# Two of the four sums of down weights, moved from the gate/up stage into the down stage; accumulating transfers in turn; GpSimd without ordered waits on VectorE

## The chip, the cores and the metric

The kernel runs on one core of one Trainium2 chip. The metric is the device time of an execution in microseconds (us). The kernel before takes 2027.6 us, the median of three runs (2026.89 to 2027.85).

The engines are called as the profile calls them: PE is TensorE (matmul), PEld its weight loads, DVE is VectorE, ACT is ScalarE, POOL is GpSimd, and SP is the engine whose queue issues most DMA transfers.

## The reference

Two layers of a decoder trunk on 1024 tokens of width 1024, in float32. Each layer normalises, projects, runs four token mixers side by side, projects back and adds; then comes a feed-forward block of inner width 2816. The change lies in that block alone:

```python
h2 = rmsnorm(x, ffn_norm[l])
gate, up = jnp.split(h2 @ w_gate_up[l], 2, axis=-1)
x = x + (jax.nn.silu(gate) * up) @ w_down[l]
```

The accuracy asked for is that of float32.

## The kernel before, in words

**Products.** A float32 matrix is split into a high part that PE takes as it is and a low part, the rest. `split` does that: a cast on ACT for the high part, a subtraction on DVE for the low one. A product of two matrices is then three matmuls (high by high, high by low, low by high), issued by `mm3`; all matmuls of this kind have one line in the profile, L350. So each weight goes through load, cast, subtraction, matmul, in this order, and each step is an instruction on another engine.

**Seven products instead of eight.** Both products of the feed-forward block are cut into 2 x 2 blocks and done by a scheme with seven block products, named B11, B21, N1, N2, T3, T4 and B22. Each product multiplies one combination of weight blocks with one combination of activation blocks. Some combinations are blocks as they are, others are sums.

*The gate/up stage* goes through 22 column groups f. Per f, it needs sums of the gate/up weights. For f from 3 on, POOL makes them in SBUF (`GateUp.sums` and `sum4`, L1336 to L1338 and L1361). For the first three, 0, 1 and 2, they are made ahead of time in DRAM tiles `gd` by DMA transfers issued from POOL's queue, some of which add to what the destination holds (`gu_made`, L324). Layer 1's `gd` is made during layer 0's gate/up stage, one transfer per f (`next(made_next, None)`, L1705); each transfer is made to wait for the last matmul issued so far (`paced`). POOL also multiplies in the silu (L1545).

*The down stage* goes through 28 units: the seven combinations in the order B11, B21, N1, N2, T3, T4, B22, four column groups m in each. A unit is 33 matmuls. Its weight is a tile of 128 x 1408 (`Wide`: a pair of 512 columns and a half of 384). `dn_raw` issues a unit's loads two units ahead, and `dn_weights` splits them one unit ahead. The activations come back from DRAM tiles `ad`.

**Where the sums of down weights are made before.** Four of the seven combinations need a sum of the four stored blocks w0 to w3: N1 needs w2 + w3, N2 needs that and w0, T3 needs w2 + w0, B22 needs that of N2 and w1. During gate/up groups f = 4 to 19 (`DN_SUMS`), each step takes a quarter of one m: `dn_load` loads 352 columns of the four blocks, `dn_sum` makes the four sums with four POOL additions of 128 x 352 (L1623) and stores them to the DRAM tile `qd`. In the down stage, `dn_raw` reads each of the four straight from `qd`, so that POOL has nothing to do there.

**What sets the order.** The program is traced once; then the class `Order` lays out the instructions of all engines with a list of costs, chooses the order on each engine, the PSUM banks and the SBUF slots (48 pairs), tries variations, and fixes the result as a chain on each engine (`impose`). On top of that, `turns` gives many POOL additions one more wait: for the DVE operation that ends just before the addition's planned start. Any change in the program lets the planner find a new order for all of it.

Of the kernel before, what the change touches and what calls it, by code (L numbers as in the profile page):

```python
# [17 lines left out]
ALU = mybir.AluOpType  # L18
# [5 lines left out]
L = 2  # L24
HT = 512
# [9 lines left out]
B11, B21, B22, N1, N2, T3, T4, B12 = range(8)  # L35
# [93 lines left out]
def trunk_kernel(ctx: ExitStack, tc: tile.TileContext, ins, out, given=None, ends=None):  # L129
    nc = tc.nc  # L130
    act, dve, pe, pool, sp = nc.scalar, nc.vector, nc.tensor, nc.gpsimd, nc.sync
# [9 lines left out]
    R, F = View(slots, F32R), View(slots, F32)  # L141
# [155 lines left out]
    last_mm = None  # L297

    def paced(d):

        tc.add_manual_dep(
            d.ins,
            last_mm.ins.name,
            mybir.DependencyInfo(mybir.DependencyClass.Sync, mybir.DependencyReason.DATA),
            reason="pace",
        )

    def gu_made(l):

        for f in made[l]:  # L310
            w, o = ins["w_gu"][l, f], made[l][f]
            q = o.rearrange("p (n c) -> p n c", n=4)
            a11, a22, a21 = w[0, :, :HT], w[0, :, HT:], w[1, :, HT:]
            two = lambda a: a.unsqueeze(1).to_broadcast([P, 2, HT])
            for d, a, add in (
                (q[:, :2], two(a21), None),
                (o[:, : 2 * HT], w[0], ALU.add),
                (o[:, 2 * HT :], w[1], None),
                (q[:, 2:], two(a22), ALU.add),
                (q[:, 2:], two(a11), ALU.add),  # L320
                (o[:, 2 * HT : 3 * HT], a21, ALU.add),
            ):
                more = {} if add is None else {"accum_op": add}
                paced(pool.dma_start(d, a, **more))  # L324
                yield

# [193 lines left out]
    for l in range(L):  # L520
# [1010 lines left out]
        acts = {}  # L1531
        made_next = gu_made(l + 1) if l + 1 < L else iter(())
        pending = None
# [66 lines left out]
        def dn_raw(c, m):  # L1600
            w = Wide(F)
            q = {N1: 3, N2: 0, T3: 2, B22: 1}
            src = qd[m][q[c]] if c in q else ins["w_dn"][l, m, {B11: 0, B21: 1, T4: 3}[c]]
            for o, cs in zip(w.parts(), (slice(0, 2 * HT), slice(2 * HT, KW))):
                sp.dma_start(o, src[:, cs])
            return w

        CW = KW // 4

        def dn_load(n):  # L1610

            m, cs = n // 4, slice(n % 4 * CW, n % 4 * CW + CW)
            q = F.pair(), F.pair()
            for i in range(2):
                src = ins["w_dn"][l, m, 2 * i : 2 * i + 2, :, cs]
                sp.dma_start(slots.cur[q[i] // 2][:, :, :CW], src.rearrange("q p n -> p q n"))
            return m, cs, q

        def dn_sum(m, cs, q):

            w0, w1, w2, w3 = (F.ap(i + n)[:, :CW] for i in q for n in range(2))
            for o, a, b in ((w3, w2, w3), (w2, w2, w0), (w0, w3, w0), (w1, w0, w1)):
                pool.tensor_tensor(out=o, in0=a, in1=b, op=ALU.add)  # L1623
            for i in range(2):
                o = qd[m][2 * i : 2 * i + 2, :, cs]
                sp.dma_start(o.rearrange("q p n -> p q n"), slots.cur[q[i] // 2][:, :, :CW])
                F.free_pair(q[i])

# [69 lines left out]
        for f in range(3, NFF):  # L1698
# [5 lines left out]
            if l + 1 < L:  # L1704
                next(made_next, None)  # L1705
            if f % 2:
                g = f // 2
                sp.dma_start(ad_of(B11, g), F.ap(acts[2 * g][HALVES.index(0)]))
# [192 lines left out]
class Order:  # L1901
# [241 lines left out]

    def turns(self, order):

        end, _ = self.run(None, fixed=order)
        start = [x - s for x, (s, _) in zip(end, self.cost)]
        two = [k for k in order["DVE"] if self.kind[k] == "two"]
        pairs, i = [], 0
        for g in order["Pool"]:  # L2150
            if self.kind[g] != "pool":
                continue
            d = None
            while i < len(two) and end[two[i]] <= start[g] + self.LEAST:
                d = two[i]
                i += 1
            if d is not None:
                pairs.append((d, g))
        return pairs

    def trial(self, order):
# [73 lines left out]
    @staticmethod  # L2235
    def impose(tc, traced, order, turns):
        for a, b in turns:
            tc.add_manual_dep(
                traced[b],
                traced[a].name,  # L2240
                mybir.DependencyInfo(mybir.DependencyClass.Sync, mybir.DependencyReason.DATA),
                reason="turn",
            )
        for ks in order.values():
# [11 lines left out]
def scheduled_kernel(fresh, ins_of, rounds=1):  # L2256

    def trace(banks, ends, order=None, turns=()):  # L2260
        nc = fresh()
        ins, out = ins_of(nc)
        with tile.TileContext(nc) as tc:
# [6 lines left out]
            if order is not None:  # L2270
                Order.impose(tc, traced, order, turns)
        return nc, traced, asked
# [3 lines left out]
    for slow in SLOW:  # L2276
        plan, asked, first.slow = first, tried, slow
        end = plan.find()[2]
        for _ in range(rounds):
# [5 lines left out]
            order = plan.improve(best, 30)[1]  # L2285
            found.append((plan.trial(order), given, order, plan.turns(order)))
    best = min(found, key=lambda x: x[0])
    return trace(*best[1], *best[2:])[0]


# [133 lines left out]
```

## Time and profile before

| | |
|---|---|
| runs, median (lowest to highest) | 2027.6 us (2026.89 to 2027.85) |
| the profiled execution's own time | 2027.71 us |
| its span | 2025.9 us |
| granted TensorE clock, mean | 0.999 |
| bytes read from and written to HBM | 248.71 MB, 111.67 MB |
| layer 0: gate/up, down | about 390 to 793 us, 793 to 1012 |
| layer 1: gate/up, down | about 1390 to 1793 us, 1793 to 2017 |

The span runs from the first to the last instruction; the rest of the time, 1.8 us, lies around it. In a table of stretches, the columns after the stretch are its length and then, for each engine, the us it was busy and (x) how many instructions began; PEclk is the granted clock, 1.00 being full speed, and the last two are the mean busy share of the 16 DMA engines and what they moved in GB/s. In a row of a group, the mean in ns of one instruction stands behind the busy time, and behind the second bar the idle time just before the group's instructions, with what ended most of it. In a row of waits stand the total, the number and the longest. A matmul's end is modelled and overlaps the next one, so a row of PE can be 100% busy and still lose a tenth of a microsecond here and there.

### The profile page before, as it was taken

Reading aid. Unit: us, or ns where it says so; the run is one execution under the profiler, and the core shown is the slowest. Engines: PE = TensorE matmul, PEld = TensorE weight load, DVE = VectorE, ACT = ScalarE, POOL = GpSimd, SP = SyncE. Lnnn points to the kernel's source line nnn. Section 1 sums busy time; section 2 is a strip of 40 time slices with the busy share of each in tenths; the row PEclk is TensorE's granted clock in tenths of the full one; section 3 lists DMA queues with packets and bytes.
Section 4 is the critical chain, followed back from the end, with each engine's and each line's share of the span. In section 5 each row is a group of like instructions: output and inputs, shape, how many; then the busy total and the mean of one; then the engine's idle time right before and its main releaser. Section 6 shows DMA issues by size and latency. Waiting matters only on the chain.

```text
span 2025.9 us, 26778 instructions
## 1 busy us (share of the span) xinstructions
PE 2012.9 (99%) x9394; PEld 1672.9 (83%) x9394; DVE 1515.0 (75%) x2330; ACT 1026.4 (51%) x1772; POOL 529.9 (26%) x440
## 2 busy tenths in 40 slices
PE   9999999999999999999999999999999999999998
PEld 8888888888888888888888888888888888888887
DVE  8889978987667778776646898789866666676554
ACT  8457657843333335545533676677433333354343
POOL 0110000047776773000000000000577676610000
PEclk9999999999999999999999999999999999999999
DMA  6552233347666677998822133342454554487552
GB/s 209 109 105 62 72 104 112 120 154 210 203 210 197 199 210 261 386 346 299 279 75 66 48 94 127 101 154 89 164 184 165 201 172 168 163 314 250 189 177 84
DMA packets 157336, 345.91 MB, mean 171 GB/s; under 512 B 15248, under 2 KB 62480, under 8 KB 157200
## 3 DMA queue, kind: packets, MB, share of 16 engines
q1 hardware_dynamic: 150480, 326.88, 47.0%
q0 software_dynamic: 6720, 17.30, 5.2%
q8 instruction: 74, 1.21, 0.2%
q14 instruction: 62, 0.51, 0.1%
HBM read 248.71 MB, written 111.67 MB: 178 GB/s over the span
## 4 chain that ended last, share of the span: by engine, by line
PE 94%; DVE 4%; issue 1%; ACT 1%; DMA 1%; POOL 0%; DVEq 0%; SPq 0%; POOLq 0%; ACTq 0%
PE ps_mm L350 36%; PE ps_s L350 29%; PE ps_t L350 11%; PE ps_pv L350 8%; PE ps_pv L1163 2%; PE ps_t L1151 2%; PE ps_s L1093 1%; PE ps_s L1094 1%; PE ps_s L1095 1%; PE ps_s L687 1%; DVE u L373 1%; PE ps_pv L765 1%; PE ps_t L753 1%; PE ps_t L430 1%; PE ps_s L964 0%
## 5 line engine op out<-in xcount | busy, mean ns | idle before, releaser
L350 PE MATMUL ps_mm<-u,u 128*128 128x512 f32 (+1 forms) x3412 | 837.8, 389 | 1.8 <-DVE tm L451 1.2
L350 PEld LDWEIGHTS ps_mm<-u,u 128*128 128x128 f32 x3412 | 623.1, 188 | 125.4 <-DVE tm L451 2.0
L373 DVE TENSOR_TENSOR u<-u,u 128x1024 fp32r<-128x1024 f32 (+3 forms) x465 | 499.1, 1095 | 191.8 <-ACT u L370 156.6
L350 PE MATMUL ps_s<-u,u 128*128 128x512 f32 x2604 | 620.3, 389 | 0.0
L370 ACT CAST u<-u 128x1024 fp32r<-128x1024 f32 (+3 forms) x465 | 393.3, 864 | 405.6 <-DMA u<-ad 76.7
L350 PEld LDWEIGHTS ps_s<-u,u 128*128 128x128 f32 x2604 | 488.6, 188 | 102.9 <-DVE u L1412 0.6
L350 PE MATMUL ps_t<-u,u 128*128 128x512 f32 (+1 forms) x1080 | 244.9, 377 | 0.1
L350 PEld LDWEIGHTS ps_t<-u,u 128*128 128x128 f32 x1080 | 194.4, 188 | 38.0 <-DVE u L1380 0.4
L350 PE MATMUL ps_pv<-u,u 128*128 128x512 f32 x792 | 191.6, 390 | 0.2 <-ACT tm L1441 0.2
L1160 POOL MEMSET u<- 128x128 f32 x32 | 6.3, 222 | 699.6 <-PE ps_mm L350 467.8
L350 PEld LDWEIGHTS ps_pv<-u,u 128*128 128x128 f32 x792 | 148.4, 188 | 32.0 <-ACT tm L1441 0.6
L1545 POOL TENSOR_TENSOR tm<-tm,u 128x512 f32<-128x512 f32 x76 | 108.8, 1432 | 119.8 <-DVE u L373 56.8
L1543 ACT ACTIVATE tm<-tm 128x512 f32<-128x512 f32 x76 | 48.1, 633 | 131.9 <-DVE tm L451 131.9
L370 ACT CAST u<-ps_t 128x512 fp32r<-128x512 f32 (+3 forms) x132 | 64.5, 503 | 51.2 <-PE ps_t L1151 26.0
L1623 POOL TENSOR_TENSOR u<-u,u 128x352 f32<-128x352 f32 x64 | 79.4, 1242 | 29.9 <-DVE u L373 12.3
L373 DVE TENSOR_TENSOR u<-ps_t,u 128x512 fp32r<-128x512 f32 (+3 forms) x132 | 74.9, 582 | 15.0 <-ACT u L370 13.8
L1441 ACT COPY tm<-ps_s 128x512 f32<-128x512 f32 x62 | 36.3, 586 | 86.7 <-PE ps_s L350 77.5
L414 ACT ACTIVATE tm<-u 128x512 f32<-128x512 f32 (+1 forms) x91 | 53.7, 599 | 46.6 <-DVE u L1807 37.8
L324 POOL DMA_DIRECT2D gd<-in_w_gu x36 | 32.0, 889 | 167.6 <-PE ps_t L350 63.3
L375 ACT ACTIVATE u<-u,par 128x512 fp32r<-128x512 f32 x91 | 63.8, 716 | 19.4 <-DVE u L451 10.7
L451 DVE TENSOR_TENSOR tm<-tm,u 128x512 f32<-128x512 f32 x76 | 71.8, 945 | 2.2
L1623 POOL TENSOR_TENSOR u<-u 128x352 f32<-128x352 f32 x64 | 69.9, 1095 | 13.4 <-DVE u L373 6.5
(205 smaller groups left out, 2287.6 us busy)
## 6 DMA issues: line engine op xcount, KB each, us to landing
u<-in_w_gu SPq DMA_DIRECT2D x82, 512.0 KB, 3.8
ad<-u SPq DMA_DIRECT2D x154, 256.0 KB, 2.8
u<-ad SPq DMA_DIRECT2D x70, 512.0 KB, 6.1
u<-in_w_dn SPq DMA_DIRECT2D x64, 352.0 KB, 3.4
qd<-u SPq DMA_DIRECT2D x64, 352.0 KB, 2.4
u<-in_w_in SPq DMA_DIRECT2D x43, 512.0 KB, 4.7
u<-qd SPq DMA_DIRECT2D x32, 512.0 KB, 5.9
gd<-in_w_gu POOLq DMA_DIRECT2D x30, 512.0 KB, 6.8
```

The lines of the kernel that those rows point to most:

```text
L350: last_mm = pe.matmul(o, w, r, start=start and k == 0 and i == 0, stop=stop and k == n - 1 and i == 2, skip_group_check=again,)
L370: a = act.copy(hi, f)
L373: dve.tensor_tensor(out=lo, in0=f, in1=rd(hi), op=ALU.subtract)
L375: a = act.activation(hi, f, AF.Copy, scale=gain)
L414: act.activation(q, f, AF.Square)
L451: dve.tensor_tensor(out=o, in0=a, in1=b, op=ALU.mult)
L1151: pe.transpose(p[:, b * P : (b + 1) * P], pr[b][j // 4][:, (j % 4) * P : (j % 4 + 1) * P], ident,)
L1163: pe.matmul(py[:, c0:], v_of(j, h), R.ap(s)[:, c0:], start=j == 0 and n == 0, stop=j == nj - 1 and n == 1,)
L1441: act.copy(o, p)
L1543: last_silu = act.activation(g, g, AF.Silu)
L1545: pool.tensor_tensor(out=g, in0=g, in1=r, op=ALU.mult)
L1623: pool.tensor_tensor(out=o, in0=a, in1=b, op=ALU.add)
```

## The change

It does three things.

1. `dn_load` and `dn_sum` now make two of the four sums in the gate/up stage: w2 + w3 and, from it, w0 + w2 + w3. A step loads three blocks instead of four and does two additions of 128 x 352 instead of four (L1640 in the new file). The other two sums are made in the down stage: for T3 and B22, `dn_raw` loads two wide tiles instead of one, and POOL adds the second to the first in three pieces of 512, 512 and 384 columns (L1621).
2. The accumulating transfers for layer 1's `gd` go in turn: the first transfer of each of the three groups, then the second of each, and so on, instead of all six of one group after another. Each waits for the matmul that was the last one a group f earlier (`past`), not for the latest.
3. `turns` is taken out: POOL's additions no longer wait for a DVE operation unless their data or their slot asks for it.

```diff
+    def gu_made(l, past=None):
+        todo = []
         for f in made[l]:
...
-            for d, a, add in (
+            todo.append((
                 (q[:, :2], two(a21), None),
...
-                paced(pool.dma_start(d, a, **more))
-                yield
+            ))
+        for d, a, add in chain(*(zip(*todo) if past else todo)):
+            more = {} if add is None else {"accum_op": add}
+            paced(pool.dma_start(d, a, **more), past[0] if past else None)
+            yield
...
         def dn_raw(c, m):
-            w = Wide(F)
-            q = {N1: 3, N2: 0, T3: 2, B22: 1}
-            src = qd[m][q[c]] if c in q else ins["w_dn"][l, m, {B11: 0, B21: 1, T4: 3}[c]]
-            for o, cs in zip(w.parts(), (slice(0, 2 * HT), slice(2 * HT, KW))):
-                sp.dma_start(o, src[:, cs])
-            return w
+            raw, made = ins["w_dn"][l, m], qd[m]
+            srcs = {
+                B11: (raw[0],),
+                B21: (raw[1],),
+                N1: (made[3],),
+                N2: (made[0],),
+                T3: (raw[2], raw[0]),
+                T4: (raw[3],),
+                B22: (made[0], raw[1]),
+            }[c]
+            ws = [Wide(F) for _ in srcs]
+            for w, src in zip(ws, srcs):
+                for o, cs in zip(w.parts(), (slice(0, 2 * HT), slice(2 * HT, KW))):
+                    sp.dma_start(o, src[:, cs])
+            if len(ws) > 1:
+                a, b = (w.parts() for w in ws)
+                for i, cs in ((0, slice(0, HT)), (0, slice(HT, 2 * HT)), (1, slice(0, KW - 2 * HT))):
+                    pool.tensor_tensor(out=a[i][:, cs], in0=a[i][:, cs], in1=b[i][:, cs], op=ALU.add)
+                ws[1].free()
+            return ws[0]
...
-        def dn_sum(m, cs, q):
-            w0, w1, w2, w3 = (F.ap(i + n)[:, :CW] for i in q for n in range(2))
-            for o, a, b in ((w3, w2, w3), (w2, w2, w0), (w0, w3, w0), (w1, w0, w1)):
+        def dn_sum(m, cs, i0, q):
+            w0, w2, w3 = (F.ap(i)[:, :CW] for i in (i0, q, q + 1))
+            for o, a, b, n in ((w3, w2, w3, 3), (w0, w3, w0, 0)):
                 pool.tensor_tensor(out=o, in0=a, in1=b, op=ALU.add)
...
-    def turns(self, order):
...
-        for a, b in turns:
-            tc.add_manual_dep(
-                traced[b],
-                traced[a].name,
```

How it stands in the order. First POOL in layer 0's gate/up stage. Before, a piece of about one group f, with the waits each instruction has (DVE_49 is VectorE, DMAHW are transfers of SP's queue, DMASW those of POOL's own):

```order
L1623 TENSOR_TENSOR u_4955<-u_4956,u_4955 128x352 [waits DVE_49,Pool_49]
L1623 TENSOR_TENSOR u_5099<-u_5099,u_5098 128x352 [waits DMAHW7_49,Pool_49]
L1623 TENSOR_TENSOR u_4955<-u_4955 128x352 [waits Pool_49]
L1623 TENSOR_TENSOR u_5098<-u_5099,u_5098 128x352 [waits DVE_49,PE_49,Pool_49]
L1545 TENSOR_TENSOR tm<-tm,u_3719 128x512 [waits DVE_49,Activation_49]
L1361 TENSOR_TENSOR u_4901<-u_4901 128x512 [waits DVE_49]
L1623 TENSOR_TENSOR u_5098<-u_5098 128x352 [waits Pool_49]
L1336 TENSOR_TENSOR u_5194<-u_5055,u_5054 128x512 [waits DMAHW4_49,DMAHW6_49,DMAHW0_49,PE_49]
L1337 TENSOR_TENSOR u_5194<-u_5055,u_5054 128x512 [waits DVE_49]
L324 DMA gd_0_98<-in_w_gu 128x2x512 [waits DMASW5_49]
```

The same place with the change:

```order
L326 DMA gd_1_99<-in_w_gu 128x1024 [waits DMASW3_49,PE_49]
L1640 TENSOR_TENSOR u_4950<-u_4950 128x352 [waits DMAHW5_49]
L1548 TENSOR_TENSOR tm<-tm,u_3719 128x512 [waits Activation_49]
L1640 TENSOR_TENSOR u_3870<-u_4950,u_3870 128x352 [waits DMAHW1_49,DVE_49,Pool_49]
L1338 TENSOR_TENSOR u_5042<-u_4896,u_4895 128x512 [waits DMAHW3_49,DMAHW2_49,DVE_49]
L1363 TENSOR_TENSOR u_4754<-u_4754 128x512 [waits DVE_49]
L1339 TENSOR_TENSOR u_5042<-u_4896,u_4895 128x512
L1340 TENSOR_TENSOR u_4896<-u_5042,u_4895 128x512 [waits Pool_49]
```

The two sums of a step stand where four stood, and the products of the silu (L1545, now L1548) wait for ACT alone.

Second, POOL at the end of layer 0's gate/up stage. Before, the last product of the silu is followed by the next layer's work:

```order
L1545 TENSOR_TENSOR tm<-tm,u_3719 128x512 [waits DVE_49,Activation_49]
L1545 TENSOR_TENSOR tm<-tm,u_3870 128x512 [waits DVE_49,Activation_49]
L1160 MEMSET u_11175 128x128 [waits DMAHW6_49,DVE_49,PE_49]
```

With the change, the sums of the down stage stand between; here T3's last third and all of B22's, up to the next layer:

```order
L1621 TENSOR_TENSOR u_7257<-u_7257,u_8321 128x384
L1621 TENSOR_TENSOR u_8675<-u_8675,u_8676 128x512 x2
L1621 TENSOR_TENSOR u_8758<-u_8758,u_8759 128x512 x2
L1621 TENSOR_TENSOR u_8519<-u_8519,u_7741 128x384
L1621 TENSOR_TENSOR u_8834<-u_8834,u_8835 128x512 x2
L1621 TENSOR_TENSOR u_8905<-u_8905,u_8906 128x512 x2
L1621 TENSOR_TENSOR u_8519<-u_8519,u_7741 128x384
L1621 TENSOR_TENSOR u_7257<-u_7257,u_7985 128x384
L1621 TENSOR_TENSOR u_7741<-u_7741,u_8519 128x384
L1162 MEMSET u_11186 128x128 x2
```

The halves u_8519 and u_7741 come up again and again: the last thirds of three units pass through the same two places.

Third, SP's queue ahead of B22 in layer 0. Before, one load each for the first unit's pair and half, between stores (`xs`, `pho`) and loads of activations (`ad`):

```order
L1605 DMA u_8532<-qd_91 128x384
L225 DMA pho_2_8607<-u_8603 128x768
L1790 DMA xs<-u_7906 128x512
L1645 DMA u_7297<-ad_86 128x512
L1605 DMA u_8688<-qd_91 128x1024
```

With the change, a second load of the same size joins each:

```order
L1617 DMA u_8519<-qd_91 128x384 [waits DVE_49]
L1854 DMA u_7257<-xr 128x512 [waits DMAHW7_49,DVE_49]
L1617 DMA u_8675<-qd_91 128x1024 [waits DMAHW0_49,PE_49]
L1617 DMA u_8676<-in_w_dn 128x1024 [waits DMAHW1_49,PE_49]
L1656 DMA u_8726<-ad_86 128x1024 [waits DMAHW2_49,PE_49]
L1807 DMA xs<-u_8519 128x512 [waits DMAHW3_49,DVE_49]
L225 DMA pho_3_8673<-u_8669 128x768 [waits DMAHW4_49,DVE_49]
L1617 DMA u_8519<-in_w_dn 128x384 [waits DMAHW3_49,DMAHW5_49,DVE_49,Activation_49]
L220 DMA u_8750<-in_w_o 128x768 [waits DMAHW6_49,PE_49]
L1617 DMA u_8759<-in_w_dn 128x1024 [waits DMAHW7_49,DMAHW2_49,DVE_49]
```

Both operands of the first unit are loaded before PE is through with T4, and the loads of the units behind it follow between the stores.

More of the change, by code (lines that the diff above doesn't have):

```diff
@@ L1531, in trunk_kernel @@
         acts = {}
-        made_next = gu_made(l + 1) if l + 1 < L else iter(())
+        past = [last_mm]
+        made_next = gu_made(l + 1, past) if l + 1 < L else iter(())
         pending = None
@@ L1705, in trunk_kernel @@
                 next(made_next, None)
+                past[0] = last_mm
             if f % 2:
@@ L2142, in run @@
         return end, order
-    def turns(self, order):
[L2146 to L2159, printed above, removed]
     def trial(self, order):
@@ L2256, in scheduled_kernel, with trace @@
 def scheduled_kernel(fresh, ins_of, rounds=1):
-    def trace(banks, ends, order=None, turns=()):
+    def trace(banks, ends, order=None):
         nc = fresh()
@@ L2270, in trace @@
             if order is not None:
[L2271 removed]
+                Order.impose(tc, traced, order)
         return nc, traced, asked
@@ L2285, in scheduled_kernel @@
             order = plan.improve(best, 30)[1]
-            found.append((plan.trial(order), given, order, plan.turns(order)))
+            found.append((plan.trial(order), given, order))
     best = min(found, key=lambda x: x[0])
-    return trace(*best[1], *best[2:])[0]
+    return trace(*best[1], best[2])[0]
 def _constants():
```

29 lines of the change are left out of this document (11 added, 18 removed).

## The prediction

> **What bounds the kernel now.** I read the page's busy row first, then PE's stretches of 50 us, then the chain of waits, and only then the places that the change touches.
>
> ```profile
> PE 2012.9 (99%) x9394; PEld 1672.9 (83%) x9394; DVE 1515.0 (75%) x2330; ACT 1026.4 (51%) x1772; POOL 529.9 (26%) x440
> PE 94%; DVE 4%; issue 1%; ACT 1%; DMA 1%; POOL 0%; DVEq 0%; SPq 0%; POOLq 0%; ACTq 0%
> 825.16 7.48 PE ps_pv L350 x33
> ```
>
> TensorE (PE) is busy for 2012.9 of 2025.9 us, and POOL has no share of the chain that ended last. The third row is one unit of the down stage in that chain: 33 matmuls in 7.48 us, 0.2267 us each, with nothing between them. The change issues the same matmuls, so it can only fill PE's gaps or make new ones. Where the gaps are, and how many matmuls (x) a stretch holds:
>
> ```profile
> core 0: us, PE busy (x) PEld busy (x) DVE busy (x) ACT busy (x) POOL busy (x), PEclk, DMA share, GB/s
> 0.00:50.00 50.00, 48.53 (x215) 40.41 (x216) 43.46 (x73) 41.16 (x67) 1.94 (x6) 1.00 0.62 209
> ...
> 350.00:400.00 50.00, 49.59 (x216) 39.97 (x215) 48.72 (x74) 40.52 (x66) 0.00 (x0) 1.00 0.43 146
> 400.00:450.00 50.00, 49.72 (x217) 40.16 (x216) 44.76 (x59) 25.36 (x37) 18.20 (x14) 1.00 0.42 128
> 450.00:500.00 50.00, 50.00 (x223) 41.40 (x222) 36.77 (x38) 17.20 (x25) 37.75 (x28) 1.00 0.68 215
> ...
> 650.00:700.00 50.00, 49.84 (x219) 40.69 (x218) 38.74 (x35) 18.40 (x26) 39.82 (x31) 1.00 0.66 189
> ...
> 1400.00:1450.00 50.00, 49.78 (x218) 40.46 (x217) 45.05 (x61) 24.50 (x36) 17.62 (x13) 1.00 0.39 128
> 1450.00:1500.00 50.00, 50.00 (x222) 41.39 (x222) 37.21 (x39) 17.88 (x26) 35.69 (x26) 1.00 0.54 184
> ...
> 2000.00:2050.00 50.00, 16.78 (x133) 15.92 (x131) 9.52 (x19) 6.92 (x16) 0.00 (x0) 0.93 0.12 43
> ```
>
> Of the 13.0 us in which PE is idle (2025.9 - 2012.9), 1.5 lie in the first stretch (50 - 48.53) and 9.1 at the end (25.9 - 16.78), where the last results are scaled and stored. That leaves 2.4 us in the middle. A stall shorter than a matmul's modelled end doesn't show as idle, so I count matmuls too. A full stretch of the gate/up stage holds 223 (450 to 500) or 222 (1450 to 1500); 216 + 217 + 219 + 218 in the four short ones above are 18 fewer than 4 x 222, some 4.1 us. **A gain beyond 4.1 us has no row to come from**, and part of those 18 are the narrow matmuls and norms at the head of the stage, which stay.
>
> Who made PE wait, in the gate/up and down stages of layer 0 (from 420 us to 1010):
>
> ```profile
> PE ps_pv L350 <- ACT tm L1441: 0.2, 1, 0.2
> ```
>
> One wait, 0.2 us, on ScalarE. POOL is never what PE waits for.
>
> **The change part by part.** *Two sums instead of four in gate/up.* POOL's groups there:
>
> ```profile
> L1623 POOL TENSOR_TENSOR u<-u,u 128x352 f32<-128x352 f32 x64 | 79.4, 1242 | 29.9 <-DVE u L373 12.3
> L1623 POOL TENSOR_TENSOR u<-u 128x352 f32<-128x352 f32 x64 | 69.9, 1095 | 13.4 <-DVE u L373 6.5
> L1545 POOL TENSOR_TENSOR tm<-tm,u 128x512 f32<-128x512 f32 x76 | 108.8, 1432 | 119.8 <-DVE u L373 56.8
> ```
>
> 128 sums take 149.3 us in both layers; 64 of them go, some 75 us of POOL; their loads shrink by a quarter and what they store by half. What POOL is spared covers nothing on the path: PE is at 50.00 of 50.00 beside it. Worth 0.
>
> *No waits on VectorE.* POOL's waits on VectorE (the third row alone: 56.8 us) partly vanish, partly stay, since a sum still needs its data. POOL runs earlier and meets VectorE at other moments. In gate/up, by groups, from 450 to 780 us, and below it the same subtraction in the down stage, where POOL is still (822 to 972):
>
> ```profile
> L373 DVE TENSOR_TENSOR u<-u,u 128x1024 fp32r<-128x1024 f32 x54 | 90.1, 1677 | 22.1 <-ACT u L370 12.3 <-PE ps_s L350 4.3 <-DMA ad<-u 1.9
> ```
>
> ```profile
> L373 DVE TENSOR_TENSOR u<-u,u 128x1024 fp32r<-128x1024 f32 x55 | 66.6, 1224 | 34.3 <-ACT u L370 26.8 <-PE ps_mm L350 6.4 <-PE ps_t L350 0.2
> ```
>
> So beside POOL the subtraction takes 453 ns more, with the old waits in place. Fewer sums pull this down, unordered starts may push it up. The bounds for PE: a gain of at most the 4.1 us above; a loss only if VectorE's 36.77 of 50 us rise past 50, by 13 us in a stretch, and all 54 subtractions delayed by a whole 1.43 us sum instead of 0.45 would add 54 x 0.98 / 6.6 stretches = 8. No loss, then. Since no PE wait names POOL, I take a gain near the lower end: **-0.4 us**.
>
> *Accumulating transfers in turn.* POOL waited for one of them to land, and for PE:
>
> ```profile
> POOL gd L324 <- PE ps_t L350: 63.3, 8, 40.3
> POOL gd L324 <- DMA gd<-in_w_gu: 59.5, 11, 7.6
> ```
>
> In turn over three destinations, a transfer follows one on another destination, and its pace is a matmul of a group earlier: POOL's queue stands less. Behind it stand sums and products whose lateness, as said, PE does not feel; the 18 transfers are wanted only in layer 1's gate/up stage. Worth 0; bounds as for the previous part, which they share.
>
> *The sums that move into the down stage.* T3 and B22 have four units each per layer: 8 more wide loads of 128 x 1408 x 4 = 0.72 MB, 16 more DMA issues on SP (some 0.32 us each in a queue that has room), and 24 sums on POOL (512, 512 and 384 wide) per layer. A sum alone takes 1.28 us for 512, so a unit's three take an estimated 1.28 x (2 + 0.75) = 3.5 us, now between the load and the split of every such unit. What hides them is how early a unit's weights are ready. Layer 0, VectorE and PE at T3's start and at B22's:
>
> ```profile
> 504.79 1.28 POOL L1545 TENSOR_TENSOR tm<-tm,u 128x512 f32<-128x512 f32 x1 [0.79 <-ACT tm L1543]
> ```
>
> ```profile
> 905.52 2.83 DVE L373 TENSOR_TENSOR u<-u,u 128x1024 fp32r<-128x1024 f32 x3 [0.88 <-ACT u L370]
> ...
> 922.24 1.98 PE L350 MATMUL ps_s<-u,u 128*128 128x512 f32 x8
> ...
> 976.45 1.69 DVE L373 TENSOR_TENSOR u<-u,u 128x1024 fp32r<-128x1024 f32 x2 [0.25 <-ACT u L370]
> ...
> 982.08 1.30 PE L350 MATMUL ps_t<-u,u 128*128 128x512 f32 x5
> ```
>
> The split for T3's first unit ends at 908.35, 13.9 us before PE takes it. For B22's first, the 1024 wide part ends at 976.45 + 1.22 = 977.67, **4.4 us** before. 3.5 us of sums fit into both, even if nothing is loaded earlier; the second leaves 0.9. It is the narrowest place of the change. In the new order the last third of B22's later units is loaded into a half that an earlier sum must free first, which may cost a fraction of a microsecond. Bounds: 0 and the slow case below (6.3). I take the end it is nearer to: **+0.4 us**.
>
> *The bytes.* DMA from 912 to 1002 us, and its share in three stretches:
>
> ```profile
> DMA packets 9557, 25.86 MB, mean 287 GB/s; under 512 B 1065, under 2 KB 2217, under 8 KB 9552
> ```
>
> ```profile
> 852.00:882.00 30.00, 30.00 (x134) 24.86 (x133) 20.57 (x23) 15.65 (x21) 0.00 (x0) 1.00 1.02 386
> ...
> 912.00:942.00 30.00, 30.00 (x134) 24.82 (x133) 20.87 (x25) 17.29 (x22) 0.00 (x0) 1.00 0.84 291
> ...
> 972.00:1002.00 30.00, 30.00 (x134) 24.78 (x133) 22.59 (x30) 18.07 (x27) 0.00 (x0) 1.00 0.84 273
> ...
> 1912.00:1942.00 30.00, 30.00 (x134) 24.84 (x133) 16.16 (x20) 13.62 (x20) 0.00 (x0) 1.00 0.63 198
> ```
>
> 25.86 + 8 x 0.72 = 31.6 MB in 90 us are 351 GB/s. The first of these rows moved 386 with its queues full and PE at 30.00 of 30: it fits. Layer 1, at a share of 0.63, has room in any case.
>
> *The plan.* The order is found anew, so narrow stalls elsewhere may shift; bounded by the same 2.4 us of idle, either sign, taken as 0.
>
> **Sum.** The profiled execution's own time is 2027.71 us (span 2025.9 and 1.8 around it). -0.4 + 0.4 + 0 leaves 2027.7; the median of the runs lies 0.1 lower: **2027.6 us, no change**.
>
> **The rivals.** *The stalls close.* Earlier POOL work and a freer queue remove all 2.4 us of idle: 2025.2. For it: POOL's 56.8 us of waits for VectorE. Against: PE names POOL nowhere.
>
> *A sum blocks VectorE for its whole length.* For it: the POOL row at 504.79 above, and VectorE beside it:
>
> ```profile
> 504.98 3.32 DVE L373 TENSOR_TENSOR u<-u,u 128x1024 fp32r<-128x1024 f32 x2 [0.34 <-ACT tm L1543]
> ```
>
> Two subtractions took 3.32 instead of 2 x 1.22, and the 0.9 lost are most of the 1.1 us for which the POOL sum still ran. In B22's stretch of layer 0 VectorE has 22.59 us of work; four units' sums of 14.1 would make 36.7 in 30, 6.7 late, less the 4.4 of margin: +2.3, **2029.9**. [...]
>
> *DMA can't carry it (the slower side).* In the last stretch of layer 0's down stage 273 GB/s took a share of 0.84: full queues of that mix would move 273 / 0.84 = 325, not 386. Then 31.6 MB need 97.2 us, 7.2 late in 90. With 3.5 of sums behind the loads and 4.4 of margin, B22's weights come 7.2 + 3.5 - 4.4 = 6.3 us late, and PE stands: **2033.9**. For it: the share of 0.84 already there, and the fact that SP issues in order, so a late load delays all behind it. Against: the 386 just before it, at the same kind of transfers. It decides from the point where the rate there falls below 31.6 MB / (90 + 4.4 - 3.5) = 348 GB/s.
>
> *The change doesn't do what it says*, in that POOL still waits on VectorE for its data at most places: the same time as the forecast, and part of its chance.
>
> **How the numbers follow.** Forecast (2026.4 to 2028.8) 0.66; the stalls close 0.10, of which 0.03 by more than 4.1 us; VectorE blocked 0.12; DMA short 0.12. A measurement of this kernel tells about 0.2% (4.1 us) from no change. Faster by more: 0.03; slower by more: 0.12, the DMA case; within: 0.85. The range, 2025.0 to 2031.2, runs from the closed stalls past the blocked VectorE and leaves out 0.15.
>
> **What would show it.** Right: PE busy within 2 us of 2012.9 and stretches of 30 us at 134 matmuls from 792 to 1002; POOL some 75 us lighter in gate/up and some 14 us heavier in each of the two down stretches per layer; no PE wait on POOL. The blocked VectorE would show as 1024 wide subtractions near 2.4 us from 900 to 1002 and a PE wait on DVE there; the DMA case as landings of `u<-in_w_dn` and `u<-qd` near 8 us, a share near 1.0 with under 348 GB/s, and a gap of several us at B22 in layer 0. Closed stalls would show as 222 matmuls in the short stretches. The forecast is wrong if PE's idle time in the middle leaves 0 to 6 us.

## The result, and the profile after

The changed kernel takes 2032.49 us, the median of eight runs from 2029.91 to 2035.1; the kernel before took 2027.24 us beside it, with runs from 2026.55 to 2027.85. The ratio is 1.0025, 95% interval 1.0016 to 1.0033: slower by 5.2 us, outside the predicted range. The runs also lie further apart than before, 5.2 us instead of 1.3. The profiled execution is the longest of the eight: 2035.1 us, span 2033.2, which is 7.3 more than the span before. So what follows explains 7.3 us, and the median has less of it. Three executions that stand far out, of 2509 to 5248 us, are left out of the medians and ratios below.

The page's busy row and chain of the changed kernel:

```profile
PE 2014.6 (99%) x9394; PEld 1674.3 (82%) x9394; DVE 1546.8 (76%) x2330; ACT 1028.6 (51%) x1772; POOL 590.3 (29%) x424
PE 94%; DVE 2%; DMA 2%; ACT 1%; issue 1%; SPq 0%; DVEq 0%; ACTq 0%
```

PE has 1.7 us more of busy time, so most of the 7.3 us are idle. Some of the stretches of 50 us of the changed kernel:

```profile
core 0: us, PE busy (x) PEld busy (x) DVE busy (x) ACT busy (x) POOL busy (x), PEclk, DMA share, GB/s
450.00:500.00 50.00, 49.91 (x219) 40.72 (x218) 40.80 (x40) 18.08 (x25) 38.35 (x24) 1.00 0.63 195
650.00:700.00 50.00, 50.00 (x223) 41.39 (x222) 36.55 (x36) 17.70 (x24) 33.68 (x24) 1.00 0.72 188
950.00:1000.00 50.00, 45.73 (x190) 37.02 (x189) 34.68 (x41) 27.07 (x37) 13.25 (x9) 0.93 0.89 317
1450.00:1500.00 50.00, 50.00 (x222) 41.39 (x222) 42.02 (x40) 19.18 (x27) 34.79 (x22) 1.00 0.48 168
1800.00:1850.00 50.00, 50.00 (x222) 41.39 (x221) 40.29 (x45) 28.75 (x35) 3.30 (x2) 1.00 0.91 326
```

One row stands out: 950 to 1000 holds 190 matmuls where a full stretch of this stage holds 222. 32 matmuls of 0.2267 us are 7.25 us, the whole loss of this execution. The same place by PE's waits (420 to 1010 us):

```profile
PE ps_t L352 <- ACT u L372: 4.0, 1, 4.0
PE ps_mm L352 <- DVE u L1407: 0.5, 1, 0.5
PE ps_t L352 <- DVE u L375: 0.3, 1, 0.3
```

and by the chain of waits (975 to 1000 us), whose columns are the start, the length and what stood on the chain:

```profile
979.17 0.38 SPq L1617
...
979.59 3.69 DMA xs<-u
...
983.37 0.32 SPq L1854
...
983.78 0.70 SPq L1617
...
984.58 7.22 DMA u<-in_w_in
...
991.87 0.04 ACT u L237
...
992.82 0.62 ACT u L372
...
993.49 6.71 PE ps_t L352 x18
```

PE stands from 989.5 to 993.49, in the first unit of B22. It had begun that unit at 981.95, in time. Of its weights only the last third came late, by 0.3 us (the third row of the waits). What it lacks at 989.5 is the 11th activation block of B22, a tile of 128 x 512 that `dn_acts` loads into a half. This is how its load stands in SP's order (the number at the row's start left out), and POOL's sum that it waits for:

```
SP    L1617 DMA u39_7741<-in_w_dn 128x384 [waits DMAHW4_49,DMAHW0_49]
SP    ...
SP    L1661 DMA u39_7741<-ad2_86 128x512 [waits DMAHW4_49,DMAHW3_49,Pool_49]
POOL  L1621 TENSOR_TENSOR u23_8519<-u23_8519,u39_7741 128x384 [waits DMAHW4_49,DVE_49,DMAHW6_49,Activation_49,Pool_49]
```

The activation block goes into the half u39_7741, which holds the last third of the second operand of a sum, and must wait until POOL has added it. The waits of SP's queue (975 to 990 us) say how long it stood there for POOL:

```profile
SPq L1661 <- POOL u L1621: 0.5, 1, 0.5
```

The rows of these instructions, SP's and POOL's part of the timeline:

```profile
981.12 4.42 POOL L1621 TENSOR_TENSOR u<-u,u 128x512 f32<-128x512 f32 x3 [8.61 <-DVE u L378]
...
985.57 0.33 SPq L1661 DMA_DIRECT2D u<-ad  x1
...
991.87 1.04 ACT L237 CAST u<-u 128x1024 fp32r<-128x1024 f32 x1 [1.75 <-DMA u<-in_w_in]
992.82 2.08 ACT L372 CAST u<-u 128x512 fp32r<-128x512 f32 x3
```

The sums end at 985.54, the load is issued at 985.57 and takes 6.9 us to land (`u<-ad`, 256 KB, in the table of DMA issues of that stretch), so about 992.5. The cast of the next layer's weights that stands ahead on ACT (L237, ends 992.9) adds at most 0.4 us.

SP came to this load at 985.0 and waited only 0.5 us for the sum. What makes the load late is its place in SP's order, behind the sum: in the kernel before, the last activation block of B22 is asked for at 957.4 us, 28 us earlier, and lands in 5.2 us. That the planner put it there because the half comes free only then is a reading of the order, which the experiments below test. Most of the rest of the loss comes behind the wait:

```profile
993.40:996.00 2.60, 2.51 (x6) 2.03 (x7) 2.35 (x3) 2.60 (x5) 0.00 (x0) 0.50 1.01 404
996.00:998.00 2.00, 2.00 (x6) 1.52 (x6) 0.86 (x3) 0.16 (x1) 0.66 (x1) 0.50 1.05 406
...
1000.00:1002.00 2.00, 2.00 (x10) 1.65 (x9) 2.00 (x3) 0.00 (x0) 1.52 (x2) 1.00 0.67 167
```

The granted clock is 0.50 for about five us after the wait: the first eleven intervals between matmuls are 426 to 591 ns instead of 227, 2.4 us more in all.

### The profile page after: what moved, and what is told of

Read it like the earlier page. It is cut to its first block, busy times and chain, and to the rows that moved or that the text cites. A ratio compares the mean times of both kernels' runs of the same rounds, so it can differ in the third digit from the quotient of the medians.

```text
span 2033.2 us, 26773 instructions
## 1 busy us (share of the span) xinstructions
PE 2014.6 (99%) x9394; PEld 1674.3 (82%) x9394; DVE 1546.8 (76%) x2330; ACT 1028.6 (51%) x1772; POOL 590.3 (29%) x424
## 4 chain that ended last, share of the span: by engine, by line
PE 94%; DVE 2%; DMA 2%; ACT 1%; issue 1%; SPq 0%; DVEq 0%; ACTq 0%
PE ps_mm L352 38%; PE ps_s L352 27%; PE ps_t L352 11%; PE ps_pv L352 8%; PE ps_pv L1165 2%; PE ps_t L1153 2%; PE ps_s L1095 1%; DVE u L375 1%; PE ps_s L1096 1%; PE ps_s L1097 1%; DMA u<-ad 1%; PE ps_s L689 1%; PE ps_s L966 1%; PE ps_pv L767 1%; PE ps_t L755 1%; PE ps_t L432 1%
## 5 line engine op out<-in xcount | busy, mean ns | idle before, releaser
L375 DVE TENSOR_TENSOR u<-u,u 128x1024 fp32r<-128x1024 f32 (+2 forms) x465 | 544.6, 1193 | 157.7 <-ACT u L372 121.6
L372 ACT CAST u<-u 128x1024 fp32r<-128x1024 f32 (+2 forms) x465 | 393.3, 864 | 421.9 <-PE ps_mm L352 90.0
L1548 POOL TENSOR_TENSOR tm<-tm,u 128x512 f32<-128x512 f32 x76 | 124.1, 1633 | 164.8 <-ACT tm L1546 164.8
L1621 POOL TENSOR_TENSOR u<-u,u 128x512 f32<-128x512 f32 (+1 forms) x47 | 67.0, 1449 | 310.2 <-DMA u<-in_w_dn 151.1
L1363 POOL TENSOR_TENSOR u<-u 128x512 f32<-128x512 f32 x38 | 69.2, 1822 | 19.4 <-DVE u L375 19.4
L378 DVE SCALAR_TENSOR_TENSOR u<-u,par,u 128x512 fp32r<-128x512 f32 x91 | 68.7, 767 | 1.6 <-ACT u L377 1.2
```

The costliest lines, as they stand in the source:

```text
L372: a = act.copy(hi, f)
L375: dve.tensor_tensor(out=lo, in0=f, in1=rd(hi), op=ALU.subtract)
L378: dve.scalar_tensor_tensor(out=lo, in0=f, scalar=gain, in1=rd(hi), op0=ALU.mult, op1=ALU.subtract)
L1363: pool.tensor_tensor(out=q4, in0=q4, in1=F.ap(self.raw[1] + 1), op=ALU.add)
L1548: pool.tensor_tensor(out=g, in0=g, in1=r, op=ALU.mult)
L1621: pool.tensor_tensor(out=a[i][:, cs], in0=a[i][:, cs], in1=b[i][:, cs], op=ALU.add)
```

## Experiments

Every kernel below gets its own order from the planner, so I read two things from each: its time, and the place of its loss. For the place I take the start of the same numbered matmul in each profiled execution, minus its start in the kernel before (us, worked out from the traces; all kernels issue 9394 matmuls). In the kernel before, number 2400 starts at 504 us, 4000 at 868, 4400 at 959, 4800 at 1049, 6800 at 1457, the last at 2017.

```
                median   2400   4000   4400   4800   6800   last
changed         2032.5   +1.0   -0.1   -0.1   +7.1   +7.3   +7.3
p1_sums         2031.7   +1.4   +0.3   +0.3   +7.1   +6.7   +7.1
p23_only        2030.5   -0.8   -1.0   -1.0   -1.0   +2.6   +2.6
x_loads         2027.3   -0.6   -1.8   -1.8   -0.8   -0.9   -0.9
x_adds          2025.9   -0.3   -1.4   -1.4   -1.4   -1.9   -1.8
acts_early      2030.6   -0.9   -2.0   -2.0   +3.0   +2.8   +2.9
tmp_half        2031.4   +0.6   -0.5   -0.5   +3.8   +3.5   +3.6
tmp_half_acts   2027.4   -0.8   -1.9   -1.9   -1.8   -2.2   -2.2
tha_seed2       2029.1   +0.1   -1.0   -1.0   -1.0   +1.9   +2.1
seed2_after     2031.1   -0.7   -1.8   -1.8   +3.3   +4.2   +4.5
seed2_before    2030.0   -0.1   +0.4   +0.4   +0.4   +1.0   +2.2
p1_b22          2030.6   +1.8   +3.6   +3.6   +3.6   +3.2   +3.2
p1_t3           2027.6   +0.2   -0.7   -0.7   -0.7   -0.9   -0.5
layer1_only     2039.3   -1.1   +9.5   +9.5   +9.5  +12.5  +12.6
t3_free         2031.3   +0.5   -0.2   -0.2   -0.2   +2.9   +3.2
```

The kernel before, run beside them, had medians from 2027.11 to 2027.64. What to watch is the step from 4400 to 4800, the end of layer 0's down stage.

**Which part of the change.** *p1_sums*: the kernel before with the moved sums alone.

```diff
-            q = {N1: 3, N2: 0, T3: 2, B22: 1}
-            src = qd[m][q[c]] if c in q else ins["w_dn"][l, m, {B11: 0, B21: 1, T4: 3}[c]]
...
+                T3: (raw[2], raw[0]),
+                T4: (raw[3],),
+                B22: (made[0], raw[1]),
...
-            for o, a, b in ((w3, w2, w3), (w2, w2, w0), (w0, w3, w0), (w1, w0, w1)):
+            for o, a, b, n in ((w3, w2, w3, 3), (w0, w3, w0, 0)):
```

> The kernel before with part 1 alone: T3's and B22's sums are made in the down stage; the waits on VectorE and the old order of the accumulating transfers stay. Theory 'place' (the loss comes from what the moved sums bring to the down stage of layer 0: second loads, and halves of slots that they hold): 2030 to 2034 us, a PE wait of 3 to 5 us near B22's start in layer 0, none in layer 1. Rival 'waits' (the loss comes from taking out the waits on VectorE or from the transfers in turn): 2026.5 to 2028.5. Rival 'order' (any newly found order can have such a stall): a stall of some us, at another place than B22 in layer 0.

*p23_only*: the reverse of that diff on the changed kernel, so parts 2 and 3 alone.

> The changed kernel with part 1 undone: all four sums in the gate/up stage again, transfers in turn, no waits on VectorE. 'Place': 2026.5 to 2028.5, no PE wait above 1 us between 430 and 1010 us. 'Waits': 2031 to 2034. 'Order': anything from 2027 to 2033, with a stall at another place.

p1_sums took 2031.67 us, ratio 1.0022 (1.0012 to 1.0032), with the same stall at the same place:

```profile
PE ps_t L350 <- ACT u L370: 3.8, 1, 3.8
```

p23_only took 2030.45, ratio 1.0013 (1.0004 to 1.0022), and loses nothing at B22; all but 0.3 of its 3.6 us between 4800 and 6800 lie in layer 1's mixers, which the change does not touch. The loss at B22 belongs to the moved sums; removing the waits or taking turns has no part in it.

**Loads or additions.** *x_loads* loads both operands and adds nothing (T3 and B22 are computed with one operand); *x_adds* loads one operand and adds it to itself (the second operand is left out).

```diff
# x_loads
-            if len(ws) > 1:
-                a, b = (w.parts() for w in ws)
...
-                ws[1].free()
+            for w in ws[1:]:
+                w.free()
# x_adds
-                T3: (raw[2], raw[0]),
+                T3: (raw[2],),
-                B22: (made[0], raw[1]),
+                B22: (made[0],),
...
-            if len(ws) > 1:
-                a, b = (w.parts() for w in ws)
+            if c in (T3, B22):
+                a = b = ws[0].parts()
```

> The changed kernel without the additions of T3 and B22 in the down stage: both operands are still loaded, the second one is dropped unread, so T3 and B22 are computed with one operand only. Tells the second loads and the slots from the additions on POOL. If the loads (bytes in full DMA queues) make the loss: 2030 to 2034 and a stall at B22 in layer 0, with some 320 GB/s from 912 to 1002 us. If the slots that an addition holds, or VectorE blocked by it, make the loss: 2026.5 to 2028.5.

> The changed kernel with one load for T3 and B22 each and the same three additions on POOL, which add the tile to itself: the second operand of T3 and B22 is left out. If POOL's additions alone (time in the chain, VectorE blocked) make the loss: 2030 to 2034. If the loads or the second operand's slots do: 2026.5 to 2028.5, some 290 GB/s from 912 to 1002 us, and no PE wait above 1 us at B22 in layer 0.

Neither shows the stall: x_loads 2027.29 us, ratio 1.0002 (0.9993 to 1.0012), x_adds 2025.9, ratio 0.9993 (0.9984 to 1.0003). From 4400 to 4800 x_loads loses 1.0 us and x_adds nothing. The stretch of 90 us in the changed kernel, and then in x_loads:

```profile
912.00:1002.00 90.00, 85.73 (x367) 70.12 (x366) 66.06 (x76) 47.16 (x63) 22.09 (x16) 0.96 0.91 324
```

```profile
912.00:1002.00 90.00, 89.69 (x395) 73.72 (x394) 62.88 (x78) 51.59 (x70) 0.00 (x0) 1.00 0.94 341
```

x_loads moved more bytes per second than the changed kernel and PE hardly stood. So the bytes alone don't make the stall, nor do 17 additions in that stretch (x_adds: 398 matmuls, none missing). It takes both: an addition that ends late and a place that it holds. (x_adds also moves fewer bytes, 287 GB/s in that stretch; the next three runs separate that.)

**The place in SBUF.** *acts_early* lets the last activation block ask for its half ahead of B22's operands; *tmp_half* loads the last third of the second operand into a tile of the small pool `tm`, and has the planner count that transfer as a load; *tmp_half_acts* does both.

```diff
# acts_early
-            for _ in range(2):
-                if cn is not None and m < NM - 1:
+            for _ in range(3 if c == T4 else 2):
+                if cn is not None and m < (2 if c == T4 else NM - 1):
                     nxt.extend(dn_acts(cn, (len(nxt) + 1) // 2))
...
# tmp_half
-            ws = [Wide(F) for _ in srcs]
+            w = Wide(F)
+            a = w.parts()
+            b = () if len(srcs) < 2 else (F.ap2(pb := F.pair()), tmp("te")[:, : KW - 2 * HT])
...
```

> The changed kernel with one edit: T4's units issue the loads of B22's activation blocks three per unit in their first two units instead of two in the first three, so that the last block (one half of 512 columns) asks for its place in SBUF ahead of the second operands of B22's sums. Theory 'slot': in the changed kernel this load waited for the POOL addition that held its half, and PE waited for it. Then 2025.5 to 2028, no PE wait above 1 us from 960 to 1010 us, and the matmuls of the stretch come 6 to 7 us earlier than in the changed kernel. Rival 'bytes' (the queues of this stretch are too full whatever is in them): 2030 to 2034, the stall only moves to another tile of B22.

> The changed kernel, but the last third (384 columns) of the second operand of T3's and B22's sums is loaded into a tile of the small pool tm instead of a half of the common slots. Same bytes, same additions, four halves per product fewer asked for. 'Slot' (halves are scarce): under 1.5 us lost from 959 to 1049 us, 2025.5 to 2028.5. 'Bytes' (full queues make every landing late): 4 us or more lost there still, 2030 to 2034.

> Both edits: the second operand's last third in a tm tile, and the loads of B22's activation blocks issued three per unit. 'Slot': under 1 us lost from 959 to 1049 us, 2025.5 to 2027.5, and all runs close together, without the spread of 7 us that the earlier activation loads alone left. 'Bytes': 3 us or more lost there still.

acts_early took 2030.57 us (1.0011, 1.0002 to 1.0021), with runs from 2027.01 to 2034.63. The wait for the activation block is gone; the profiled run shows one 10 us later:

```profile
PE ps_mm L352 <- ACT u L372: 2.6, 2, 2.4
```

It is the last third of B22's third unit that is late, 9 of its 33 matmuls, and the chain of waits runs the same way: an `xs` store of 7.47 us, the load from `qd` that SP issues behind it, two additions, the split, PE. tmp_half took 2031.37 (1.0023, 1.0012 to 1.0033): a wait of 2.2 us at 984.6 remains, whose chain runs over two loads, 7.82 us of `u<-ad` and 4.92 us of `u<-in_w_o`. My 'slot' theory was wrong in expecting that either edit alone would do, and both times the numbers came as the rival 'bytes' had them. With both, 2027.42 us (1.0001, 0.9991 to 1.001), and nothing missing from 912 to 1002:

```profile
912.00:1002.00 90.00, 90.00 (x398) 74.32 (x397) 78.01 (x85) 54.37 (x74) 26.75 (x17) 1.00 0.92 334
```

The same sums and the same loads at 334 GB/s against 324, so the bytes alone are not the cause again: the halves were, or more exactly the order in which loads must wait for them. The issue of B22's last activation block says it for all kernels. It is at 985.6 us in the changed kernel, 985.9 in p1_sums and 982.6 in seed2_after (below), the three in which PE waits for this block. It is at 957.4 in the kernel before, 949.8 in acts_early, 958.0 in tmp_half and 954.0 in tmp_half_acts and x_adds, and at 973.8 in x_loads. Either edit alone brings this load back; the waits that then remain are for other tiles.

The runs of tmp_half_acts still spread from 2025.5 to 2029.78, against my expectation that they would be close, and the profiled one is the fastest, so a stall there in the slower ones is not excluded. The version does not beat the kernel before.

**Is it one order?** *seed2_after* and *seed2_before* change `random.Random(1)` to `random.Random(2)` in the planner's `improve`, *tha_seed2* does so in tmp_half_acts.

> The changed kernel with another start value for the planner's trials, so another order of the same work. 'Slot' as a matter of the change: 2029.5 to 2034 with a PE wait of 2 us or more near B22's start in layer 0. 'Order' (the stall belongs to one found order): 2026 to 2029, no such wait; other places differ by up to 3 us in either direction.

> The kernel before with another start value for the planner's trials. Measures what a newly found order alone does to this kernel: if the mixers' stages react as in the kernel with part 1 undone, 2025 to 2031; if orders of the same program agree, 2026.5 to 2028.5. No PE wait above 1 us at B22 in layer 0 by either.

> The version with both edits (second operand's last third in a tm tile, activation loads three per unit), with the planner's other start value. If freeing the halves cures the place whatever the order: under 1.5 us lost from 959 to 1049 us, 2026 to 2029. If the cure was one lucky order: 3 us or more lost there, 2030 to 2034.

seed2_after took 2031.12 (1.002, 1.0011 to 1.003) and stalls at the same unit. Here the chain of waits names the sum and the issue of the load:

```profile
981.59 1.03 POOL u L1621
...
982.63 0.33 SPq L1661
...
983.01 6.69 DMA u<-phin
989.70 0.01 issue
989.70 0.62 ACT u L372
...
990.37 1.91 PE ps_t L352 x5
```

POOL's addition, the issue of the activation load on SP (L1661), a transfer, the cast, PE. The transfer in the chain is that of the next load, `phin`, which SP issued at 983.01; the activation load itself, issued at 982.63, took 6.7 us too and landed at 989.3, and the cast followed at 989.70, behind that of L237. SP stood 0.3 us for the sum. tha_seed2 took 2029.09 (1.0008, 0.9998 to 1.0017) and loses 0.0 us from 4400 to 4800, in a profiled execution of 2029.91 us, above its median: stall and cure both outlast a new order. seed2_before took 2030.0, ratio 1.0011 (1.0002 to 1.0021), 2.5 us more than the same program in its first order, most of it in the two gate/up stages. So a new order by itself moves this kernel by some 2.5 us. In the second order the change costs 1.1 us (2031.12 against 2030.0), with intervals that overlap, and in the first 5.2: the times could not have told the change from the order; the place can, for the stall at B22 is there in both orders of the changed kernel and in neither of the kernel before.

**Which product, which layer.** Only one product's sum is moved in *p1_b22* and *p1_t3* (part 1, with the waits on VectorE) and in *t3_free* (T3, with parts 2 and 3); *layer1_only* is the changed kernel with layer 0's sums left in the gate/up stage.

```diff
+        moved = ((), (T3, B22))[l]
...
-                T3: (raw[2], raw[0]),
+                T3: (raw[2], raw[0]) if T3 in moved else (made[2],),
...
-                B22: (made[0], raw[1]),
+                B22: (made[0], raw[1]) if B22 in moved else (made[1],),
```

> Part 1 alone (as before, with the waits on VectorE), but only B22's sum is moved into the down stage; T3's stays in the gate/up stage. If B22's place in layer 0 makes the loss by itself: 2029.5 to 2034, with a PE wait of 2 us or more between 975 and 1010 us and 5 to 7 us lost between the matmuls at 959 and 1049 us. If the loss needs T3's loads ahead of it: under 1.5 us lost there, 2027 to 2030 with what a new order does elsewhere.

> Part 1 alone, but only T3's sum is moved into the down stage; B22's stays in the gate/up stage. T3 had 13.9 us of margin in the kernel before, and its sums run ahead of T4: under 1.5 us lost between 868 and 1049 us, no PE wait above 1 us there, and 2026 to 2030 with what a new order does elsewhere. If any moved sum brings the stall: 2 us or more lost at T3 or behind it.

> The changed kernel (transfers in turn, no waits on VectorE), but only T3's sum is moved into the down stage; B22's is made in the gate/up stage. Against the same with the waits (2027.6). 'Slot': no loss from 868 to 1049 us. If taking the waits out is worth the 1 to 2 us that the changed kernel gained in the gate/up stage: 2025.5 to 2027. If unordered POOL additions block VectorE when three sums stand there (as with four sums in layer 0): 2 us or more lost from 413 to 777 us, 2029 and more.

> The changed kernel with T3's and B22's sums moved into the down stage in layer 1 alone; layer 0 makes all four in the gate/up stage as before. 'Slot' and 'bytes' alike: no stall at B22 in layer 0, none in layer 1 where the next layer's loads are missing: 2025.5 to 2028.5, but for what the order does to the mixers (up to 3 us). If the loss were in layer 1 or in the waits taken out: 2030 and more.

p1_t3 took 2027.57 (1.0003, 0.9994 to 1.0012), p1_b22 2030.62 (1.0017, 1.0007 to 1.0027); neither loses anything at B22, in one order each. p1_b22's 3.6 us are gone by matmul 4000, 2 of them at one wait on ScalarE at 762 us (`ACT tm L1441`, 1.8 us). So in these orders the stall needs both products. In p1_b22 the last activation block is asked for at 980.6 us, also late, but it lands in 4.5 us instead of 6.9, and PE does not wait for it. That T3's second operands take up the halves just ahead of B22's fits; how much of the difference is their bytes is not separated. t3_free took 2031.31 (1.0019, 1.0009 to 1.003), with no loss in the gate/up stage (+0.5 to -0.2) and 3.1 us from 4800 to 6800, nearly all in layer 1's mixers, like p23_only.

layer1_only took 2039.34 us, ratio 1.0057 (1.0042 to 1.0072), far from my 2025.5 to 2028.5. Nothing is lost at B22 and 0.1 us from 6800 on, as expected, and 3.0 us from 4800 to 6800, but 10.6 us in layer 0's gate/up stage, where four sums now stand without waits on VectorE. PE's two longest groups of waits in the whole execution:

```profile
PE ps_t L352 <- DVE u L1540: 4.2, 2, 2.4
PE ps_s L352 <- DVE tm L1784: 2.3, 1, 2.3
```

VectorE there, from 500 to 780 us, and the same group in the kernel before:

```profile
L1557 DVE TENSOR_TENSOR u<-u,u 128x512 f32<-128x512 f32 x7 | 14.6, 2081 | 0.1
```

```profile
L1554 DVE TENSOR_TENSOR u<-u,u 128x512 f32<-128x512 f32 x7 | 9.1, 1293 | 2.6 <-DMA qd<-u 1.7 <-POOL u L1623 0.8
```

One instruction of this group takes 2081 ns on average instead of 1293. p23_only has the same sums without waits in that stage and loses nothing there. That the additions beside this group lengthen it is my guess, and no run shows it; what sets the two orders apart I have not settled.

## Why the prediction was wrong

**The step that failed** is the term of the moved sums, "+0.4 us": it asked only whether a unit's own weights come in time, and put the other loads that use the halves at nothing without a reason. The part that it did count came in the size it gave: the last third of the weights, whose sum goes through such a half, cost PE 0.3 us, "a fraction of a microsecond", though in B22's first unit and not a later one. The right kind of wait was named, but for the wrong tile. The activation block goes through a half too; its load was asked for at 985.57 instead of 957.4 and landed some 3 us after PE had stopped for it. That cost a wait of 4.0 us and 2.4 us of half clock behind it, 6.7 us with the 0.3, where the term had 0.4. To its wait for the place the load added its landing, 6.9 us.

The length of the sums was too small as well: the three in front of that load took 4.42 us and not 3.5. The 3.5 went by one row of 1.28 us for 512 columns; in the down stage such a sum took 1.56 us on average. And two of the three belong to B22's second unit: POOL's order puts its wide pieces ahead of the first unit's last third, whose half the activation block waits for.

**The bytes.** The rival that DMA can't carry it gave 2033.9, near the measured 2032.5 and the profiled 2035.1, and some of its signs came: 324 GB/s, under my 348, landings of `u<-in_w_dn` at 7.1 us in that stretch, a gap at B22. But the bytes were not the cause by themselves, and the near number is luck: tmp_half_acts needs the same transfers and loses nothing at 334. What the higher rate (324 GB/s against 287) may have added is the landing of the late block, 6.9 us against 5.2 before. My bound of 348 GB/s was wrong too, since the planner moved part of the transfers out of those 90 us (29.20 MB moved there, not 31.6). That SP issues in order, as the rival had it, shows in the changed kernel: an `xr` load (L1854) waited 1.7 us for an `xs` store, and SP issued nothing from 981.6 to 983.4 us. Layer 1 had room, as said: from matmul 6800 to the last the changed kernel loses nothing.

**A sum blocks VectorE.** Not in the down stage: 1024 wide subtractions took 1367 ns from 900 to 1002 us against 1225 before, not 2.4 us, and PE's longest wait for VectorE from 900 on there was the 0.3 us above. In the gate/up stage the same group (450 to 780 us) went

```profile
L375 DVE TENSOR_TENSOR u<-u,u 128x1024 fp32r<-128x1024 f32 x54 | 97.8, 1820 | 11.6 <-PE ps_s L352 5.5 <-ACT u L372 3.8 <-DMA qd<-u 1.8
```

from 1677 ns to 1820, although 34 of the 201 POOL instructions of that stage (392 to 792 us) were gone; with the sums halved and the waits kept (p1_sums) it was 1500. PE lost nothing by it, as I had argued.

**POOL 75 us lighter in gate/up** was wrong: 258.93 us in layer 0 from 392 to 792 became 247.72, and in layer 1 it did not fall. The 64 sums went, but what stayed takes longer:

```profile
L1548 POOL TENSOR_TENSOR tm<-tm,u 128x512 f32<-128x512 f32 x76 | 124.1, 1633 | 164.8 <-ACT tm L1546 164.8
L1363 POOL TENSOR_TENSOR u<-u 128x512 f32<-128x512 f32 x38 | 69.2, 1822 | 19.4 <-DVE u L375 19.4
L1640 POOL TENSOR_TENSOR u<-u 128x352 f32<-128x352 f32 x32 | 50.4, 1574 | 35.9 <-DMA u<-in_w_dn 35.9
```

1633 ns instead of 1432 in the first, 1822 instead of 1501 in the second, 1574 instead of 1095 in the third. For the second and the third that goes with the waits: p1_sums, with the sums halved and the waits kept, has 1371 and 1018 ns. For the silu products of the first it does not, for p1_sums has them longer still:

```profile
L1545 POOL TENSOR_TENSOR tm<-tm,u 128x512 f32<-128x512 f32 x76 | 135.3, 1780 | 156.5 <-ACT tm L1543 86.5 <-DVE u L373 66.4 <-DVE u L1537 1.8
```

What lengthened these is open.

**The gain of 0.4 us** in the gate/up stage came as some 1.1 (from matmul 2400 to 4000), but not from the step that forecast it. 0.7 of it lies between matmuls 3000 and 3100, where PE of the kernel before stalls twice for some tenths of a microsecond, at 649 and 660 us. Every other kernel but layer1_only gains these 0.7, seed2_before among them, which has neither fewer sums nor fewer waits: they belong to the first order of the kernel before. The 0.4 that are left come in p1_sums, with the waits in place, and not in p23_only, without them. That the sum fits is luck.

**The plan at 0, bounded by 2.4 us.** seed2_before shows 2.5 us for a new order alone. I should have carried that into the range at both ends. By the sign that the prediction gave itself it is wrong too: of the 18.6 us in which PE is idle 1.7 lie in the first stretch and 9.1 at the end, which leaves 7.8 in the middle, not 0 to 6.

## What to carry to other kernels

Where loads, operands and results share one pool of places, ask of a new operand not only whether its own work fits, but which load gets its place next and how long that load takes to land; two transfers through one place are a chain even where bandwidth is left (PE stood at 324 GB/s here, and 334 ran without a stall). Cost a PE wait with what follows it, here 2.4 us behind a wait of 4.0. And where a planner lays out everything anew, time a second order of the same program first: here it moved the kernel by half of what the change did.

## What the runs showed that I had not expected

In these traces PE's granted clock went to 0.50 at seven of its waits; at two little shorter ones no such stretch followed. The seven, as intervals between the starts of two matmuls, were of 2.60 to 4.37 us: two in layer1_only and one each in the changed kernel, p1_sums, acts_early, tmp_half and seed2_after. Matmuls at 427 ns instead of 227 followed each of them and cost 1.7 to 2.5 us more (worked out from the traces). After the two of 2.19 and 2.22 us only the first matmul was slow (341 and 337 ns). Two of layer1_only, after 2.80 us and after 2.22 us:

```profile
658.50:661.00 2.50, 2.42 (x7) 1.93 (x8) 2.50 (x5) 1.64 (x2) 0.00 (x0) 0.62 0.91 227
738.40:741.00 2.60, 2.54 (x11) 2.12 (x12) 2.60 (x5) 1.64 (x2) 0.00 (x0) 1.00 0.55 206
```

The second row has the granted clock at 1.00, the first at 0.62. So of these nine late tiles two cost little beyond their wait and seven 1.7 us or more. This may be part of why the changed kernel's runs lie 5 us apart: the granted clock was 0.997 or 0.998 in the six runs from 2030.6 us up and 0.999 in the two at 2029.9.

The clock did not fall at the same point in each. In the changed kernel, the first of the two below, it fell 2.2 us into the wait, which began at 989.5, and stayed at 0.50 for 6.8 us; in seed2_after it fell 0.7 us after PE had begun again at 990.37:

```profile
989.50:991.70 2.20, 0.01 (x1) 0.00 (x0) 1.36 (x2) 0.62 (x2) 1.07 (x1) 1.00 0.99 354
991.70:998.50 6.80, 5.01 (x12) 3.95 (x13) 3.71 (x5) 4.76 (x7) 2.70 (x3) 0.50 1.01 399
998.50:1002.00 3.50, 3.50 (x17) 2.89 (x16) 3.50 (x4) 0.77 (x2) 3.02 (x3) 1.00 0.63 189
```

```profile
990.40:991.10 0.70, 0.70 (x3) 0.61 (x4) 0.70 (x2) 0.70 (x2) 0.13 (x1) 1.00 1.03 397
991.10:994.50 3.40, 3.40 (x9) 2.62 (x9) 2.71 (x4) 2.12 (x4) 0.00 (x0) 0.50 1.02 380
```

What decides whether and when it falls is not shown: these are nine waits, and no run varies the length of one alone.
